# A list scheduler that orders a two-layer diffusion backbone 126 times instead of once, easing TensorE's longest pause each time

## The chip, the cores and the metric

One core of one Trainium2 chip runs the whole program. The metric is the device time of one execution in microseconds (us); the number that counts is the median of several runs. Engines are named as in the profile: PE is TensorE's matrix multiplication, PEld its weight load, DVE VectorE, ACT ScalarE, POOL GpSimd, SP the engine that issues all the transfers here.

## What is computed

A hybrid backbone of two layers over 512 latent and 256 context tokens of width 1024. Cut to what matters:

```python
for l in range(2):
    m_lat, m_ctx = silu(c) @ ada_w[l] + ada_b[l], silu(c_ctx) @ ada_w[l] + ada_b[l]     # 9 x 1024 each
    x, ctx = ffn_sublayer(x, m_lat[:, 0:3], ...), ffn_sublayer(ctx, m_ctx[:, 0:3], ...)  # FFN1
    mix_lat, mix_ctx = token_mix(modulate(x, ...), modulate(ctx, ...), w_in[l], w_out[l], ...)
    x = layer_norm(ALPHA * x + m_lat[:, 5] * mix_lat, ln_g[l, 1], ln_b[l, 1])
    x = ffn_sublayer(x, m_lat[:, 6:9], ...)                                              # FFN2
    # the context goes the same way in layer 0 alone
def modulate(x, shift, scale):  return layer_norm(x) * (1 + scale) + shift
def ffn_sublayer(x, m, w_gu, w_down, g, b):
    g_, u = split(modulate(x, m[0], m[1]) @ w_gu, 2)                                     # 1024 -> 2 x 2816
    return layer_norm(ALPHA * x + 0.5 * m[2] * (silu(g_) * u) @ w_down, g, b)
```

`token_mix` projects once (`w_in`) into three groups: grouped-query attention with RMS norm and rotation (A), a Hyena long convolution (B) and latent attention (C); their outputs are joined and projected by `w_out`.

## The kernel before

The tokens lie in six tiles of 128 (four latent, two context). Every 32-bit operand of the large products is split in two: a rounded part `hi`, cast by ACT, and the rest `lo`, subtracted by DVE or POOL; `mm3` then issues three matmuls (hi·hi, hi·lo, lo·hi). Weights come in tiles of 128x1024 through `weights`: SP loads `raw`, ACT casts `hi`, DVE subtracts `lo`.

Between two sublayers stands a path that no product can pass. `post` (L555) multiplies the output in PSUM with the gate and adds it to the residual (DVE, POOL), then normalises: `stats` (L507) takes `bn_stats` and `bn_aggr` on DVE and then a chain of 12 DVE steps on 128x2 values, variance plus epsilon, the ten steps of `rsqrt` (L490) and `nmr` (minus mean times the reciprocal root), each of which needs the one before. Two `scalar_tensor_tensor` of 128x1024 per tile apply it. `pre` (L535) then does `stats` again, with a second such chain, `norms` (L527) on ACT, transposes on PE, scale and shift on ACT, cast `Hhi` on ACT, and the rest `Hlo` on POOL. In the second half of layer 1 the latent tokens go through this in two groups of two tiles; the first three column blocks of FFN2 are made by `lat(..., cut=2)`, 144 matmuls of 128x256 for the first group and then 144 for the second.

Nothing is issued in the order in which the program names it. All engines are stand-ins (`_Engine`, L396) that record each operation with its dependencies and a cost by a formula (`cost`); this is why every instruction of the profile has the line L347. `order` then makes a list schedule: each engine in turn takes, of the operations that are ready by the modelled times, the one that comes first in the program. It models latencies between engines, the buffers of each pool (`_Slots`), the SBUF port that VectorE and GpSimd share (`shares`, `port`), and groups of matmuls that should stay together. `issue` emits the instructions in that order, and every engine keeps to it: an instruction that is not ready holds up all that stand behind it.

## Time and profile before

| | |
|---|---|
| median of 3 runs (lowest to highest) | 2902.86 us (2902.28 to 2903.89) |
| the profiled execution: its time, its span | 2903.62 us, 2901.2 us |
| PE busy, share of the span | 2812.3 us, 97% |
| DVE, ACT, POOL busy | 1716.4, 1006.4, 566.3 us |
| mean granted TensorE clock | 0.987 of 2.4 GHz |

The span is the time from the first to the last instruction of the execution, 2.4 us less than its device time. PE does nearly all the work, so that time lies in two things: pauses of PE (2901.2 less 2812.3, 88.9 us) and stretches in which its matmuls ran at 1.2 GHz (granted clock 0.5) instead of 2.4.

### The profile page before, as it was taken

The numbers are of one execution on the slowest core, as the hardware profiler recorded it, in microseconds if no ns is written. First come the engines' busy times: TensorE is split into PE (matmuls) and PEld (weight loads), VectorE is DVE, ScalarE is ACT, GpSimd is POOL, SyncE is SP. The second block draws the span as 40 slices with busy tenths as digits, with TensorE's granted clock in tenths as the row PEclk, the third lists the DMA queues.
The fourth block names the chain that finished last, engine by engine and source line by source line (L and its number), as shares of the span: only waits on it lengthen the run. The fifth ranks groups of instructions, "written<-read, shape, count | busy, mean of one in ns | idle before, by whom it ended". The sixth has DMA issues, their size and how long they took to land.

```text
span 2901.2 us, 41228 instructions
## 1 busy us (share of the span) xinstructions
PE 2812.3 (97%) x16132; PEld 2416.2 (83%) x16132; DVE 1716.4 (59%) x3485; ACT 1006.4 (35%) x1988; POOL 566.3 (20%) x545
## 2 busy tenths in 40 slices
PE   7999999999999999999999899999999999799998
PEld 5888888889887898888888788888889778688886
DVE  7887566286677663556626953653257677623335
ACT  4212222246657452121123421212217658432221
POOL 3201123125020031013311210122115220210220
PEclk9999999999999999999999999999999999899999
DMA  8654344121111313333321342431212113133231
GB/s 284 227 172 142 120 128 130 61 91 60 37 62 45 103 57 108 106 117 124 115 75 69 118 147 72 129 101 59 81 59 100 49 44 102 52 106 98 88 116 66
DMA packets 105714, 291.36 MB, mean 100 GB/s; under 512 B 15184, under 2 KB 17392, under 8 KB 105520
## 3 DMA queue, kind: packets, MB, share of 16 engines
q1 hardware_dynamic: 105520, 288.73, 30.7%
q8 instruction: 127, 2.08, 0.3%
q14 instruction: 67, 0.55, 0.1%
HBM read 277.23 MB, written 11.45 MB: 100 GB/s over the span
## 4 chain that ended last, share of the span: by engine, by line
PE 63%; DVE 5%; ACT 2%; issue 1%; POOL 0%; DVEq 0%; ACTq 0%; POOLq 0%
PE p L347 63%; DVE u L347 2%; DVE s L347 2%; ACT t L347 1%; DVE w L347 1%; DVE t L347 1%; ACT u L347 0%; ACT Hhi L347 0%; ACT w L347 0%; DVE Hlo L347 0%; DVE junk L347 0%; DVE adaw L347 0%; POOL Hlo L347 0%; ACT L347 0%; DVEq L1661 0%
## 5 line engine op out<-in xcount | busy, mean ns | idle before, releaser
L347 PE MATMUL p<-Hhi,w 128*128 128x256 f32 (+1 forms) x5536 | 1363.3, 337 | 9.3 <-ACT Hhi L347 6.1
L347 PEld LDWEIGHTS p<-Hhi,w 128*128 128x128 f32 x5536 | 953.8, 191 | 121.2 <-ACT Hhi L347 8.4
L347 PE MATMUL p<-Hlo,w 128*128 128x256 f32 (+1 forms) x2768 | 929.8, 336 | 0.1
L347 PE MATMUL p<-w,u 128*128 128x512 f32 x2904 | 665.7, 390 | 0.0
L347 DVE TENSOR_TENSOR w<-raw,w 128x1024 fp32r<-128x1024 f32 (+2 forms) x312 | 393.0, 1261 | 441.7 <-PE p L347 312.2
L347 PEld LDWEIGHTS p<-w,u 128*128 128x128 f32 x2904 | 543.7, 188 | 112.1
L347 ACT CAST w<-raw 128x1024 fp32r<-128x1024 f32 (+2 forms) x312 | 323.1, 1043 | 742.9 <-PE p L347 605.8
L347 PEld LDWEIGHTS p<-Hlo,w 128*128 128x128 f32 x2768 | 527.2, 191 | 53.8 <-issue 1.4
L347 POOL TENSOR_TENSOR u<-t,u 128x512 fp32r<-128x512 f32 (+1 forms) x154 | 185.7, 1206 | 1259.7 <-ACT u L347 1207.0
L347 DVE TENSOR_TENSOR t<-t,p 128x512 f32<-128x512 f32 (+1 forms) x160 | 90.9, 568 | 420.6 <-PE p L347 389.0
L347 PE MATMUL p<-u,u 128*64 128x128 f32 (+7 forms) x2120 | 277.4, 323 | 19.3 <-ACT t L347 5.2
L347 POOL TENSOR_TENSOR u<-u,t 128x512 f32<-128x512 f32 (+2 forms) x128 | 165.4, 1320 | 500.5 <-DVE t L347 366.7
L347 PEld LDWEIGHTS p<-u,u 128*64 128x64 f32 (+4 forms) x2120 | 202.8, 160 | 69.7 <-issue 27.0
L347 ACT CAST u<-t 128x512 fp32r<-128x512 f32 (+1 forms) x154 | 81.2, 528 | 410.4 <-DVE t L347 410.4
L347 DVE SCALAR_TENSOR_TENSOR junk<-adaw,crow 128x512 bf16<-128x512 f32 x256 | 209.5, 818 | 19.5 <-DMA adaw<-in_ada_t 18.6
L347 DVE SCALAR_TENSOR_TENSOR adaw<-adaw,crow 128x512 f32<-128x512 f32 x256 | 216.1, 844 | 7.0
L347 PE MATMUL p<-w,Hhi 128*128 128x416 f32 (+3 forms) x712 | 194.0, 354 | 6.7 <-ACT w L347 6.7
L347 DVE TENSOR_TENSOR t<-p,u 128x512 f32<-128x512 f32 x196 | 131.5, 686 | 91.2 <-PE p L347 90.1
L347 ACT ACTIVATE t<-p 128x512 f32<-128x512 f32 (+2 forms) x162 | 79.8, 495 | 291.2 <-PE p L347 286.9
L347 PEld LDWEIGHTS p<-w,Hhi 128*128 128x128 f32 x712 | 130.0, 193 | 18.3 <-ACT w L347 7.8
L347 PE MATMUL p<-ident,t 128*128 128x128 f32 x848 | 121.9, 282 | 22.2 <-ACT t L347 17.5
L347 POOL TENSOR_TENSOR Hlo<-t,Hhi 128x512 fp32r<-128x512 f32 x72 | 95.5, 1336 | 244.5 <-ACT Hhi L347 244.3
(122 smaller groups left out, 2181.2 us busy)
## 6 DMA issues: line engine op xcount, KB each, us to landing
raw<-in_ffn_gu SPq DMA_DIRECT2D x176, 512.0 KB, 3.6
adaw<-in_ada_t SPq DMA_DIRECT2D x256, 256.0 KB, 2.9
raw<-in_ffn_down SPq DMA_DIRECT2D x88, 512.0 KB, 3.6
raw<-in_w_out_u SPq DMA_DIRECT2D x16, 512.0 KB, 3.4
u<-in_x_all SPq DMA_DIRECT2D x12, 512.0 KB, 7.9
xs<-u SPq DMA_DIRECT2D x12, 512.0 KB, 2.7
raw<-in_w_hy SPq DMA_DIRECT2D x12, 512.0 KB, 3.3
u<-grow SPq DMA_DIRECT2D x10, 512.0 KB, 4.8
```

Source lines behind the costliest of these rows:

```text
L347: getattr(getattr(self.nc, eng), method)(*args, **kw)
```

## The change

The instructions of each engine are the same in number and kind. New is how often they are ordered, and what an order may do:

- `tune` makes the first schedule as before. Then it takes the longest modelled pause of TensorE above 150 ns (`gaps`) that it has not yet tried, and `hurry` walks back from the matmul that ends it, along what each operation waited for last, at most 12 us. For an operation on the way that was ready and had to wait over 60 ns for its engine it (1) gives it a priority ahead of those that ran in its way; (2) notes, in `behind`, big operations that had begun before it was ready, which must now come after it; (3) where the way leads through a chain of `stats`, adds this chain to `held`: once begun, VectorE takes nothing else until its 12 steps are done.
- Each such try is a new schedule: the priorities alone, the chains alone, all together. One is kept if the modelled end is earlier, up to 125 tries.
- `stats` keeps the scratch of `rsqrt` in the same tile as its other values (five columns per tile instead of four and a small tile of its own), and notes the chain by `nc.chain`.

```diff
+    PAUSE, BACK = 150.0, 12000.0
...
+    def chain(self, n0):
+        for n in range(n0, len(self.ops)):
+            self.chains[n] = n0
...
+    def gaps(self):
+        last, res = 0.0, []
+        for t, n in sorted((self.starts[n], n) for n, op in enumerate(self.ops) if op[0] == "tensor"):
+            if t - last > self.PAUSE:
+                res.append((t - last, n))
+            last = max(last, t + self.ops[n][6])
+        return sorted(res, reverse=True)
...
+    def hurry(self, n, prio, behind, held):
+        p, q, h, since = None, None, None, self.starts[n] - self.BACK
+        while n is not None and self.starts[n] > since:
+            t, r = self.starts[n], self.ready[n]
+            c = self.chains.get(n)
+            if c is not None and c not in held:
+                h = (h or held) | {c}
+            if t - r > 60.0:
+                x = prio[n]
+                for m in reversed(self.ran[self.ops[n][0]][:self.place[n]]):
+                    if self.starts[m] + self.ops[m][6] <= r:
+                        break
+                    x = min(x, prio[m] - 0.5)
+                    if self.starts[m] < r - 20.0 and self.ops[m][6] > 400.0 and self.ops[m][0] != "tensor":
+                        q = q or {k: [*v] for k, v in behind.items()}
+                        q.setdefault(n, []).append(m)
+                if x < prio[n]:
+                    p = p or [*prio]
+                    p[n] = x
+            n = self.cause[n]
+        return p or prio, q or behind, h or held
...
+    def tune(self, tries):
+        state = lambda: (self.end, self.starts, self.ready, self.cause, self.place, self.ran)
+        self.fixed = self.setup()
+        gc.disable()
+        now = [*map(float, range(len(self.ops)))], {}, frozenset()
+        res = self.order(*now)
+        kept = state()
+        done = set()
+        while tries > 0:
+            for _, n in self.gaps():
+                if n not in done:
+                    break
+            else:
+                break
+            done.add(n)
+            p, q, h = self.hurry(n, *now)
+            seen = [now]
+            for new in ((p, now[1], now[2]), (now[0], now[1], h), (p, q, h)):
+                if new in seen:
+                    continue
+                seen.append(new)
+                tries -= 1
+                r = self.order(*new)
+                if r and self.end < kept[0]:
+                    res, kept, now = r, state(), new
+                    done.discard(n)
+                    break
+                self.end, self.starts, self.ready, self.cause, self.place, self.ran = kept
+        gc.enable()
+        return res
...
-                if avail[e]:
+                    n = heapq.heappop(future[e])[1]
+                    heapq.heappush(avail[e], (prio[n], n))
+                if e == "vector" and hold is not None:
+                    t0 = max(when[e], ready[hold])
+                elif avail[e]:
...
+            if e == "vector" and hold is not None:
+                n = hold
+                avail[e].remove((prio[n], n))
+                heapq.heapify(avail[e])
+            else:
+                n = heapq.heappop(avail[e])[1]
...
-            if shares[n]:
+            if shares[n] and (e != "vector" or hold is None):
...
+            self.ready[n] = ready[n]
             for tag, r in opens[n]:
+                t1 = slots[tag].free[0]
+                if t1 > self.ready[n]:
+                    self.ready[n], cause[n] = t1, freed.get((tag, t1))
...
+                c = self.chains.get(n)
+                hold = n + 1 if c in held and self.chains.get(n + 1) == c else None
...
+            for m in behind.get(n, ()):
                 need[m] -= 1
...
     def issue(self):
-        for n in self.order():
+        for n in self.tune(125):
...
-    def rsqrt(self, y, v, t):
+    def rsqrt(self, y, v, t, p=None):
...
-        p = self.small(v.shape[-1])
+        if p is None:
+            p = self.small(v.shape[-1])
...
-        r = self.small(4 * n)
-        v, y, t, nmr = [r[:, n * i:n * i + n] for i in range(4)]
+        r = self.small(5 * n)
+        v, y, t, nmr, p = [r[:, n * i:n * i + n] for i in range(5)]
+        n0 = len(nc.ops)
         nc.vector.tensor_scalar(v, var, EPS, None, ALU.add)
-        self.rsqrt(y, v, t)
+        self.rsqrt(y, v, t, p)
         nc.vector.scalar_tensor_tensor(nmr, mean, -1.0, y, ALU.mult, ALU.mult)
+        nc.chain(n0)
         return [[x[:, j:j + 1] for x in (y, nmr, mean)] for j in range(n)]
```

What moves is seen in the order of the engines' instructions. In it the lines of the changed file are other ones (L465 for L347), and the numbers of the tiles are lower, since the scratch tiles are no longer named.

First, VectorE at the end of layer 1's token mix, where the first two latent tiles are normalised: s_3652 holds their mean and variance, s_3655 and s_3656 the chain's values; t and p with the numbers 367x are the gate's products of the other two tiles, w_3698 and w_3701 the `lo` parts of FFN2's weights. Before:

```order
L347 BN_AGGR s_3652<-s_3654 128x2
L347 TENSOR_SCALAR s_3655<-s_3652 128x2
L347 SCALAR_TENSOR_TENSOR u_3616<-u_3616,s_3652,u_3614 128x1024
L347 TENSOR_SCALAR s_3655<-s_3655 128x2
L347 SCALAR_TENSOR_TENSOR u_3617<-u_3617,s_3652,u_3614 128x1024
L347 TENSOR_SCALAR s_3655<-s_3655 128x2
L347 TENSOR_TENSOR t_3672<-p_3670,u_3613 128x512
L347 TENSOR_TENSOR s_3655<-s_3655 128x2
L347 SCALAR_TENSOR_TENSOR s_3655<-s_3655 128x2
L347 TENSOR_TENSOR w_3698<-raw_3696,w_3697 128x1024
L347 SCALAR_TENSOR_TENSOR s_3655<-s_3655 128x2
L347 BN_STATS s_3679<-u_3618 128x6
```

The same place now (the mean and variance are s_3625, the chain s_3628):

```order
L465 BN_AGGR s_3625<-s_3627 128x2
L465 TENSOR_SCALAR s_3628<-s_3625 128x2
L465 TENSOR_SCALAR s_3628<-s_3628 128x2 x2
L465 TENSOR_TENSOR s_3628<-s_3628 128x2
L465 SCALAR_TENSOR_TENSOR s_3628<-s_3628 128x2 x2
L465 TENSOR_TENSOR s_3628<-s_3628 128x2 x2
L465 TENSOR_SCALAR s_3628<-s_3628 128x2
L465 TENSOR_TENSOR s_3628<-s_3628 128x2
L465 SCALAR_TENSOR_TENSOR s_3628<-s_3628 128x2
L465 SCALAR_TENSOR_TENSOR s_3628<-s_3625,s_3628 128x2
L465 SCALAR_TENSOR_TENSOR u_3589<-u_3589,s_3625,u_3587 128x1024
L465 SCALAR_TENSOR_TENSOR u_3590<-u_3590,s_3625,u_3587 128x1024
```

The 12 steps stand in one piece, with what stood between them behind. The second chain of the same two tiles stands in one piece too, ahead of the other tiles' work and of the six weights' subtractions.

Second, PE at the same place: p_3675 (now p_3646) is the last of `w_out`'s sums, the matmuls with `ident` are the transposes of the first two tiles (t_3657, t_3658; now t_3629, t_3630), p_3702 the first sum of FFN2. Before:

```order
L347 MATMUL p_3675<-u_3648,Hhi 128x512
L347 MATMUL p_3675<-u_3649,Hhi 128x512
L347 MATMUL p_3675<-u_3648,Hlo 128x512
L347 MATMUL p_3665<-ident_83,t_3657 128x128 x4
L347 MATMUL p_3668<-ident_83,t_3658 128x128 x3
L347 MATMUL p_3666<-ident_83,t_3657 128x128 x4
L347 MATMUL p_3668<-ident_83,t_3658 128x128
L347 MATMUL p_3669<-ident_83,t_3658 128x128 x4
L347 MATMUL p_3702<-Hhi,w_3697 128x256
```

Now:

```order
L465 MATMUL p_3646<-u_3618,Hlo 128x512
L465 MATMUL p_3636<-ident_83,t_3629 128x128 x4
L465 MATMUL p_3646<-u_3618,Hhi 128x512
L465 MATMUL p_3639<-ident_83,t_3630 128x128 x4
L465 MATMUL p_3646<-u_3619,Hhi 128x512
L465 MATMUL p_3637<-ident_83,t_3629 128x128 x4
L465 MATMUL p_3646<-u_3618,Hlo 128x512
L465 MATMUL p_3640<-ident_83,t_3630 128x128 x4
L465 MATMUL p_3646<-u_3621,Hhi 128x512
```

The transposes stand among the last matmuls of `w_out`'s sum, nine of which follow the first four transposes, and no longer behind them all.

Third, VectorE in layer 1's input projection, where q of group A gets its RMS norm (the 128x12 values s_3138 to s_3141) and is scaled (t_3133): w_3242 and w_3289 are `lo` parts of weights, t_3157 a piece of Hyena's short convolution. Before:

```order
L347 TENSOR_SCALAR s_3139<-s_3139 128x12
L347 TENSOR_TENSOR w_3242<-raw_3240,w_3241 128x1024
L347 TENSOR_TENSOR s_3140<-s_3138,s_3139 128x12
L347 SCALAR_TENSOR_TENSOR t_3157<-p_3158,convw_3010,t_3157 128x511
L347 SCALAR_TENSOR_TENSOR s_3140<-s_3140,s_3139 128x12
L347 SCALAR_TENSOR_TENSOR t_3157<-p_3158,convw_3010,t_3157 128x511
L347 SCALAR_TENSOR_TENSOR s_3139<-s_3140,s_3139 128x12
L347 TENSOR_TENSOR s_3140<-s_3138,s_3139 128x12
```

Now:

```order
L465 TENSOR_SCALAR s_3112<-s_3112 128x12
L465 TENSOR_TENSOR s_3113<-s_3111,s_3112 128x12
L465 SCALAR_TENSOR_TENSOR s_3113<-s_3113,s_3112 128x12
L465 SCALAR_TENSOR_TENSOR s_3112<-s_3113,s_3112 128x12
L465 TENSOR_TENSOR s_3113<-s_3111,s_3112 128x12
```

The convolution's two pieces stand behind the scaling of q, and the subtraction of w_3242 (now w_3215) ten instructions further back still.

Two more places are spoken of below. On SP the first 512 KB of the modulation's weights (adaw_160) are loaded first of all and not fifteenth. And in the last 290 us of the program, all of FFN2 in layer 1 but its beginning, no engine's order changes.

## Rows read from the trace of the kernel before

**Rows 1.** The page: busy time of PE, and its busy tenths and clock in 40 slices.

```profile
PE 2812.3 (97%) x16132; PEld 2416.2 (83%) x16132; DVE 1716.4 (59%) x3485; ACT 1006.4 (35%) x1988; POOL 566.3 (20%) x545
...
PE   7999999999999999999999899999999999799998
...
PEclk9999999999999999999999999999999999899999
```

**Rows 2.** What PE waited for: us in total, times, longest.

```profile
PE p L347 <- ACT t L347: 26.6, 20, 10.3
PE p L347 <- DMA adaw<-in_ada_w: 10.1, 1, 10.1
```

**Rows 3.** Stretches: length; busy PE, PEld, DVE, ACT, POOL; clock, DMA share, GB/s.

```profile
0.00:45.00 45.00, 26.13 (x182) 13.11 (x182) 34.60 (x93) 23.87 (x38) 8.44 (x13) 1.00 0.87 312
636.00:662.00 26.00, 23.02 (x138) 21.19 (x137) 12.78 (x28) 20.52 (x51) 13.82 (x15) 0.94 0.17 64
850.00:950.00 100.00, 93.66 (x696) 77.74 (x694) 81.31 (x172) 63.34 (x179) 16.31 (x19) 0.98 0.15 48
1052.00:1593.00 541.00, 541.00 (x2997) 472.74 (x2997) 278.36 (x518) 135.56 (x215) 101.97 (x80) 1.00 0.30 98
1593.00:1645.00 52.00, 42.42 (x267) 36.04 (x266) 47.44 (x122) 28.67 (x60) 12.98 (x10) 0.87 0.30 94
...
2245.00:2300.00 55.00, 49.08 (x295) 40.27 (x293) 40.69 (x76) 31.77 (x70) 18.33 (x17) 0.91 0.19 64
2380.00:2436.00 56.00, 50.60 (x371) 40.57 (x371) 43.45 (x87) 38.01 (x100) 3.18 (x6) 0.95 0.15 48
2488.00:2548.00 60.00, 45.23 (x274) 41.23 (x273) 36.65 (x88) 28.00 (x54) 13.76 (x10) 0.83 0.14 45
2885.00:2901.00 16.00, 4.96 (x22) 3.75 (x20) 12.22 (x39) 0.00 (x0) 0.00 (x0) 0.80 0.26 98
```

**Rows 4.** PE's timeline, token mix to FFN2: start, us, instruction, count [idle before <-releaser].

```profile
2516.82 3.68 PE L347 MATMUL p<-ident,t 128*128 128x128 f32 x16 [10.28 <-ACT t L347]
2524.99 1.65 PE L347 MATMUL p<-Hhi,w 128*128 128x256 f32 x6 [4.49 <-ACT Hhi L347]
...
2529.81 0.36 PE L347 MATMUL p<-Hhi,w 128*128 128x256 f32 x1
...
2531.17 0.28 PE L347 MATMUL p<-Hlo,w 128*128 128x256 f32 x1
```

**Rows 5.** DVE's timeline at the same place.

```profile
2488.18 0.17 DVE L347 TENSOR_SCALAR s<-s 128x2 f32<-128x2 f32 x1
2488.26 1.28 DVE L347 SCALAR_TENSOR_TENSOR u<-u,s,u 128x1024 f32<-128x1024 f32 x1
...
2497.92 1.27 DVE L347 TENSOR_TENSOR s<-s,s 128x2 f32<-128x2 f32 x1
...
2502.46 2.47 DVE L347 BATCH_NORM_STATS2 s<-u 128x6 f32<-128x512 f32 x4
...
2516.17 0.36 DVE L347 TENSOR_TENSOR s<-s 128x2 f32<-128x2 f32 x2
```

**Rows 6.** ACT's timeline at the same place: `norms` of the first and second group.

```profile
2515.95 2.93 ACT L347 ACTIVATE t<-u,s 128x512 f32<-128x512 f32 x4 [12.63 <-DVE s L347]
...
2526.81 2.94 ACT L347 ACTIVATE t<-u,s 128x512 f32<-128x512 f32 x4 [0.17 <-DVE s L347]
```

**Rows 7.** POOL's timeline at the same place.

```profile
2496.93 2.24 POOL L347 TENSOR_TENSOR u<-u,t 128x512 f32<-128x512 f32 x1 [4.02 <-ACT w L347]
```

**Rows 8.** DVE's timeline, layer 1's projection: a weight's subtraction inside q's RMS chain.

```profile
2254.65 1.23 DVE L347 TENSOR_TENSOR w<-raw,w 128x1024 fp32r<-128x1024 f32 x1 [0.57 <-PE p L347]
```

**Rows 9.** PE's timeline where the scores of group A begin.

```profile
2279.67 1.19 PE L347 MATMUL p<-u,u 128*128 128x512 f32 x2 [3.86 <-DVE s L347]
```

**Rows 10.** DVE's timeline between layer 0 and layer 1: one step of a chain of `stats`.

```profile
1619.71 1.11 DVE L347 TENSOR_SCALAR s<-s 128x2 int32<-128x2 int32 x1
```

**Rows 11.** POOL's timeline at that step.

```profile
1619.54 1.26 POOL L347 TENSOR_TENSOR Hlo<-t,Hhi 128x512 fp32r<-128x512 f32 x1 [0.65 <-ACT Hhi L347]
```

More of the change, by code (lines that the diff above doesn't have):

```diff
@@ L1 @@
+import gc
 import heapq
@@ L67, in __init__ @@
         self.pools = {}
-        self.group = {}
+        self.group, self.chains = {}, {}
         for e in ("tensor", "vector", "scalar", "gpsimd", "sync"):
@@ L199, in shares @@
         return (two or bool(aps)) and not any(x.space == PSUM for x in args if isinstance(x, bass.AP))
-    def order(self):
+    def gaps(self):
[26 more added lines that the diff above has]
+        return p or prio, q or behind, h or held
@@ L202, in order, with setup @@
+    def setup(self):
         ops = self.ops
@@ L234, in order @@
                     opens[first[t]].append((tag, r))
-                slots[tag] = _Slots(tag[2], seq, self.AHEAD.get(tag[1], 16))
+                slots[tag] = tag[2], seq, self.AHEAD.get(tag[1], 16)
+        shares = [self.shares(*op[:4]) for op in ops]
+        return succ, need, left, opens, slots, rank, shares
+    def order(self, prio, behind, held):
+        ops = self.ops
+        N = len(ops)
+        cause = self.cause = [None] * N
+        self.ready = [0.0] * N
+        self.place = [0] * N
+        ran = self.ran = {e: [] for e in ("tensor", "vector", "scalar", "gpsimd", "sync")}
+        freed = {}
+        succ, need, left, opens, slots, rank, shares = self.fixed
+        need, left = [*need], {**left}
+        slots = {tag: _Slots(*x) for tag, x in slots.items()}
+        for n, ms in behind.items():
+            for m in ms:
+                need[m] += 1
         ends = {}
@@ L242, in order @@
         quiet, cold = -1e9, 0.0
-        tied = None
+        tied = hold = None
         port = {"vector": 0.0, "gpsimd": 0.0}
-        shares = [self.shares(*op[:4]) for op in ops]
         starts = self.starts = [0.0] * N
@@ L273, in order @@
                     best = (t0, e)
+            if best is None:
+                return None
             t0, e = best
@@ L276, in order @@
             while future[e] and future[e][0][0] <= t0:
[L277 to L278 removed]
+                n = heapq.heappop(future[e])[1]
+                heapq.heappush(avail[e], (prio[n], n))
+            if e == "vector" and hold is not None:
[4 more added lines that the diff above has]
+                n = heapq.heappop(avail[e])[1]
             if e == "tensor" and tied is not None and self.group.get(n) != tied:
[L281 to L283 removed]
+                for x in avail[e]:
+                    if self.group.get(x[1]) == tied:
+                        avail[e].remove(x)
                         heapq.heapify(avail[e])
[L285 to L286 removed]
+                        heapq.heappush(avail[e], (prio[n], n))
+                        n = x[1]
                         break
[L288 removed]
+            if shares[n] and (e != "vector" or hold is None):
                 free = port["gpsimd" if e == "vector" else "vector"]
@@ L292, in order @@
                     passed = [n]
-                    while avail[e] and len(passed) < 12 and shares[avail[e][0]]:
-                        passed.append(heapq.heappop(avail[e]))
-                    m = heapq.heappop(avail[e]) if avail[e] and not shares[avail[e][0]] else None
+                    while avail[e] and len(passed) < 12 and shares[avail[e][0][1]]:
+                        passed.append(heapq.heappop(avail[e])[1])
+                    m = heapq.heappop(avail[e])[1] if avail[e] and not shares[avail[e][0][1]] else None
                     for x in passed[m is None:]:
-                        heapq.heappush(avail[e], x)
+                        heapq.heappush(avail[e], (prio[x], x))
                     if m is not None:
@@ L307, in order @@
             res.append(n)
+            self.place[n] = len(ran[e])
+            ran[e].append(n)
             if shares[n]:
@@ L326, in order @@
                 lat = 0.0 if e == f == "tensor" else self.LAT["same" if e == f else "tensor" if "tensor" in (e, f) else "cross"]
-                ready[m] = max(ready[m], done + lat)
+                if done + lat > ready[m]:
+                    ready[m], cause[m] = done + lat, n
+                need[m] -= 1
+                if not need[m]:
+                    offer(m)
+            for m in behind.get(n, ()):
                 need[m] -= 1
@@ L336, in order @@
                     slots[tag].give(rank[t], ends[t] + self.LAT["cross"])
+                    freed[tag, ends[t] + self.LAT["cross"]] = n
                     wake.append(tag)
```

9 lines of the change are left out of this document (1 added, 8 removed).

## Prediction

> **What bounds the kernel now.** I read the page first: PE is busy for 97% of the span, its tenths are full nearly everywhere, and its clock is full but for one slice [rows 1]. So the kernel is bound by TensorE's own work, and a new order can only win what PE loses: 88.9 us of pauses (2901.2 - 2812.3) and the matmuls that ran at half clock. The second view, what PE waited for, says which pauses an order can reach: the largest sum, 26.6 us in 20 waits, is for ACT's `t`, the end of the path through the norms, while 10.1 us are one wait for the first weights by DMA [rows 2]. The third view, stretches, places them [rows 3]. In 1052 to 1593 PE has no pause at all, and the other long stretches between the rows look the same. Idle PE time (length less busy) is 18.9 us at the start, 3.0 in 636:662, 6.3 in 850:950, 9.6 in 1593:1645, 5.9 in 2245:2300, 5.4 in 2380:2436, 14.8 in 2488:2548 and 11.0 at the end. The clock tells of more: at 0.83 of 2488:2548, one third of that stretch was at 1.2 GHz (0.5) and the rest at 2.4.
>
> **The change, place by place.** Durations are of the profiled execution, 2903.62 us, 0.76 above the median; the sum is made against it.
>
> *Token mix to FFN2 in layer 1 (14.8 us idle).* Before, the first chain begins at 2488.18, each of its steps separated by foreign work of up to 1.28 us, and the four `bn_stats` behind it begin at 2502.46: 14.3 us [rows 5]. Held, 12 steps take 2.4 us (two steps take 0.36 and the next starts 0.39 after the first [rows 5], so 0.2 each), the four applications 4 x 1.2 = 4.8 us (1.28 each with 0.08 of overlap [rows 5]), so `bn_stats` begins at 2488.2 + 7.2 = 2495.4 and ends 2.4 later. Two aggregates and two gate products stand before the second chain (about 1.7 us by their like in these rows, an estimate), then 2.4 us of chain: `norms` starts at 2501.9, not at 2515.95 [rows 6], 14.0 us earlier. The first transposes could then run at 2516.8 - 14.0 = 2502.8 [rows 4], while `w_out`'s sum is still running; the wait of 10.28 goes. From the start of `norms` to FFN2's first matmul it took 9.04 us (2524.99 - 2515.95), through ACT and POOL, which stay: FFN2 starts at about 2511.0.
> What is late next is the second group. Its DVE work stands behind the chains and the six subtractions as before, so I leave its `norms` at 2526.8 [rows 6]; its first matmul then comes 9.04 later, at 2535.9. The first group's 144 matmuls at 0.12 us (0.36 from one triple to the next at full clock, behind [rows 4]) and 16 transposes at 0.09 last 18.7 us, to 2529.7: a new pause of 6 us. Before, the same work from 2524.99, its first 4.4 us at half clock, ended near 2546. The gain is 2546 - 2536 = 10, less 1 for a half-clock stretch behind the new pause: **-9** (bounds -5, if the chains meet POOL as told below and the second group comes later by what now passes it, and -12, if that group gains too).
>
> *Scores of group A in layer 1 (5.9 us idle, clock 0.91).* On DVE a subtraction of 1.23 us [rows 8] and two convolution pieces of 0.7 leave the RMS chain, so q is scaled 2.7 us earlier, and two more subtractions leave the time in which POOL rotates q. PE's wait of 3.86 [rows 9] is for what hangs on this. Convolution matmuls of later blocks are now fill between the scores. At clock 0.91, 0.18 of 55 us ran at half speed, 9.9 us, worth up to 5. I take **-6**; bounds -2 (2.7 less a stall of 0.7 at the transposes, which stand earlier) and -8.4 (all idle time and half the clock).
>
> *Layer 0 to layer 1 (9.6 us idle, clock 0.87).* The second of two chains is held; the first is not, and its 4 us stay. The `lo` subtraction that PE waited 2 us for comes earlier. **-4.4**; bounds -1 and -8.
>
> *FFN1 to token mix in layer 0 (3.0 us idle, clock 0.94).* The chain is held; at most 3.0 + 1.6 of clock. **-3.5**; bounds -1.5 and -4.5.
>
> *Small pauses in the attention of both layers (6.3 and 5.4 us).* Fill is moved in between them; half of 11.7: **-6**; bounds 0 and -10.
>
> *Unchanged.* Order is kept in the 541 us at full load and in the long stretches like it, and at the end (11.0 us idle). At the start the two DMA waits of 10.1 and 4.9 us stay in sum: one load of 512 KB passes the others at the 312 GB/s of that stretch [rows 3], 1.7 us that the others land later, while its own matmuls come earlier. I take 0, bounds -2 and +3.
>
> *What it costs.* PE changes between forms of operands 597 times and no longer 568, counted over its order. Where one matmul of a triple stands alone behind transposes, its successor starts 0.20 after it and not 0.12 (2529.81 and behind it [rows 4]): 29 x 0.08 = **+2.3**, bounds 0 and +3.
>
> Sum: -9 - 6 - 4.4 - 3.5 - 6 + 2.3 = -26.6; 2903.6 - 26.6 = 2877.0, at the median 2876.3. I forecast **2876 us**.
>
> **A rule that speaks against holding.** At 1619.71 a step on two values per partition takes 1.11 us, while POOL runs an operation from 1619.54 to 1620.80 [rows 10, 11]; at 2497.92 one takes 1.27, inside POOL's 2.24 [rows 5, 7]. Such a step takes 0.16 to 0.2 otherwise. So a held chain does not run at 0.2 us a step where POOL works, and DVE, kept from all other work, waits with it.
> The Trainium skill (SBUF — State Buffer, "SBUF: two separate sides") says the same as a mechanism: VectorE's operations with two SBUF inputs, or in a two-port mode, and GpSimd's share one pair of ports as an exclusive lock, and the loser is blocked for the whole operation of the other. By that rule alone no step of a chain is safe from POOL, and the sum would be that of the first rival; by the rows only steps that meet a POOL operation pay, and I take two of these on the path of the -9.
>
> **Rivals.**
> 1. *POOL stops the held chains, and the kernel gets slower.* Place: the four held chains on PE's path (two at 2488, one each in 636:662 and 1593:1645). Each blocked step costs 1.27 - 0.16 = 1.1 us; all 12 are 13.2 a chain, 53 in all, against a gain of 26.6: 2929. It decides at half of them, six blocked steps a chain (24 steps, 26.4 us). For it: four POOL operations lie in the chain's time in each of the two earlier places (15 and 10 in those whole stretches [rows 3]). Against it: between them POOL pauses for 0.65 us [rows 11], time for three steps, so that four operations block about four steps; and the interleaved chains of before paid for the same locks.
> 2. *What is gained is waited for at the next place.* The second group of FFN2, the rope of the A heads and the unheld chain each keep their time, and only the first part of each gain counts: -5, -2, -1, -1.5 and -1 are -10.5; with +2.3 the kernel is at 2894. For it: the new pause of 6 us is of this kind already. Against: 144 matmuls are a cover of 17 us.
> 3. *The pauses and the half-clock stretches behind them go altogether:* -12 - 8.4 - 8 - 4.5 - 10, with +2.3 and -2 at the start: -42.6, 2860. For it: 125 tries, each kept only if it helps the model; against it: ACT's and POOL's 9 us from `norms` to the first matmul stay in any order, and so does a pause behind each of them that finds no other work.
> 4. *Nothing measurable:* the order is shaped to modelled times, and where an operation comes later than modelled, PE, which takes its matmuls in order, stands before it with ready work behind. 2903.
>
> **How the numbers follow.** 0.2%, 5.8 us, is about what a measurement of this kernel tells from no change. Forecast 0.59, second rival 0.18 (a sixth of it within 0.2%), third 0.11, fourth 0.05, first 0.07. Faster 0.59 + 0.15 + 0.11 = 0.85, same 0.03 + 0.05 = 0.08, slower 0.07. The range reaches from 2856, a little below the third rival, to 2896, above the second; it leaves out the first and fourth and the tail of each side.
>
> **What would show it.** In the profile of the changed kernel: PE's longest wait behind the start no longer 10.28 for ACT's `t`, but one of 4 to 7 us between the two groups of FFN2; 12 chain steps in about 2.4 us at 2488, with at most two over 1 us; FFN2's first matmul under 6 us behind the end of `w_out`'s sum, not 18.5 (2524.99 less 2516.82 - 10.28); the wait of 3.86 at the scores under 1; the clock in the slice at 2500 above 0.9; the last 11 us as before. The forecast is wrong if a held chain takes over 6 us at 2488, if the transposes among `w_out`'s last matmuls hold PE for more than 3 us, or if the start takes 3 us more.

## The result and the profile after

The changed kernel takes **2873.68 us** (2872.49 to 2874.53, 4 runs) against 2902.57 (2901.67 to 2903.89, 4 runs): ratio 0.990, 95% interval 0.9883 to 0.9917, or 28.9 us less. The forecast was 2876.0, its range 2856 to 2896. The total came out as forecast; two of its terms did not, and two more lie a little past their bounds.

The page of the changed kernel, the lines of [rows 1] (lines of code are now L465):

```profile
PE 2803.5 (98%) x16132; PEld 2410.0 (84%) x16132; DVE 1721.2 (60%) x3485; ACT 1006.6 (35%) x1988; POOL 563.7 (20%) x545
...
PE   7999999999999999999999999999999999899998
...
PEclk9999999999999999999999999999999999999999
```

The span is 2871.7 us, so PE now pauses for 68.2 us and not 88.9: 20.7 of the 29.5 us by which the span shrank. The other 8.8 are PE's busy time, 2812.3 less 2803.5, with the same 16132 matmuls. The clock accounts for it: its mean rose from 0.987 to 0.991, and PE spent about 75 us of the span at 1.2 GHz before (0.013 x 2901.2 / 0.5) and about 52 now (0.009 x 2871.7 / 0.5). So nearly a third of the gain is matmuls that no longer run at 1.2 GHz.

What PE waited for, after:

```profile
PE p L465 <- ACT t L465: 17.1, 14, 4.8
PE p L465 <- ACT u L465: 8.8, 3, 7.8
PE p L465 <- DMA u<-in_hy_z: 6.5, 1, 6.5
PE p L465 <- ACT Hhi L465: 5.6, 2, 3.9
```

The largest sum is still for ACT's `t`, but 17.1 and not 26.6, and the longest of them is 4.8 and not 10.3 [rows 2]. Stretches of after, cut where the same work stands as in [rows 3], the first 45 us left for below:

```profile
639.30:660.60 21.30, 20.86 (x134) 19.82 (x132) 13.20 (x25) 18.94 (x47) 11.22 (x12) 1.00 0.19 72
848.30:944.40 96.10, 92.15 (x696) 76.45 (x694) 80.09 (x171) 63.51 (x179) 15.71 (x19) 1.00 0.15 48
1045.40:1586.50 541.10, 541.10 (x2998) 472.80 (x2997) 281.72 (x531) 130.79 (x202) 97.02 (x76) 1.00 0.31 98
1586.50:1633.20 46.70, 40.11 (x265) 34.91 (x264) 39.30 (x105) 27.88 (x60) 11.55 (x9) 0.85 0.30 94
2234.40:2276.00 41.60, 38.91 (x210) 31.34 (x209) 31.91 (x57) 23.89 (x46) 16.31 (x17) 1.00 0.27 84
2355.60:2409.60 54.00, 51.53 (x392) 42.03 (x390) 43.37 (x87) 38.44 (x99) 5.42 (x8) 1.00 0.15 50
2461.60:2518.50 56.90, 47.25 (x278) 42.58 (x277) 40.73 (x87) 27.56 (x54) 13.49 (x10) 0.89 0.14 47
2855.50:2871.50 16.00, 5.00 (x23) 3.79 (x21) 12.26 (x39) 0.00 (x0) 0.00 (x0) 0.78 0.26 98
```

The full stretch (1045 to 1586) and the end are as before. In four places the clock is 1.00 where it was 0.94, 0.98, 0.91 and 0.95. Two places still run at 0.85 and 0.89. Not all of this is the change's: in run 1 below, whose order on PE, DVE, ACT and POOL is that of before, the clock between 850 and 950 is 1.00 as well.

**Where the time went, place by place.** I matched every matmul of the two traces and took the difference of its start at points of PE's order behind which the same set of matmuls stands in both. What the difference grows by between two points is what that place gave:

| place (us of before) | forecast (bounds) | measured |
|---|---|---|
| start, to 97 | 0 (-2 to +3) | +3.3 |
| FFN1 to token mix, layer 0 (620 to 665) | -3.5 (-4.5 to -1.5) | -4.7 |
| small pauses, attention of layer 0 (850 to 950) and layer 1 (2375 to 2450) | -6 (-10 to 0) | -3.9 and -6.4 |
| layer 0 to layer 1 (1593 to 1656) | -4.4 (-8 to -1) | -5.3 |
| scores of A, layer 1 (2245 to 2310) | -6 (-8.4 to -2) | -7.7 |
| token mix to FFN2, layer 1 (2486 to 2561) | **-9 (-12 to -5)** | **-3.0** |
| changes between operand forms | +2.3 (0 to +3) | not seen apart |
| rest: -0.3 (665 to 850), -0.9 (at 1050), +1.2 (at 2181), -1.8 (2310 to 2375) | 0 | -1.8 |
| sum, against the profiled execution (measured: its span) | -26.6 | -29.5 |

Between 2260 and 2389 the order has no common point; there I gave each matmul's own gain to its place in before, so the split of these 13.6 us into -7.7, -1.8 and -4.1 is an estimate, their sum is not. The table sets one execution against one. How much a place changes without any change of order is seen in run 1: -0.7 between 620 and 665, -1.4 between 850 and 950, under 0.3 at each other place behind the start.

**Token mix to FFN2.** DVE's timeline of after; a row with xN puts N like instructions together:

```profile
2461.73 0.58 DVE L465 TENSOR_SCALAR s<-s 128x2 f32<-128x2 f32 x3
...
2463.92 0.16 DVE L465 SCALAR_TENSOR_TENSOR s<-s,s 128x2 f32<-128x2 f32 x1
2464.00 4.87 DVE L465 SCALAR_TENSOR_TENSOR u<-u,s,u 128x1024 f32<-128x1024 f32 x4
...
2472.49 2.33 DVE L465 TENSOR_SCALAR s<-s 128x2 f32<-128x2 f32 x3
...
2482.54 2.12 DVE L465 TENSOR_TENSOR w<-raw,w 128x1024 fp32r<-128x1024 f32 x1
2484.57 1.75 DVE L465 TENSOR_TENSOR u<-u,t 128x512 f32<-128x512 f32 x1
2486.24 2.30 DVE L465 TENSOR_TENSOR w<-raw,w 128x1024 fp32r<-128x1024 f32 x1
...
2489.07 1.69 DVE L465 TENSOR_TENSOR w<-raw,w 128x1024 fp32r<-128x1024 f32 x1
...
2501.51 0.58 DVE L465 TENSOR_SCALAR s<-s 128x2 f32<-128x2 f32 x3
```

POOL's timeline at the same place, and ACT's (`norms` of the two groups):

```profile
2472.05 2.54 POOL L465 TENSOR_TENSOR u<-u,t 128x512 f32<-128x512 f32 x2 [21.79 <-DVE s L465]
2482.30 1.27 POOL L465 TENSOR_TENSOR Hlo<-t,Hhi 128x512 fp32r<-128x512 f32 x1 [7.71 <-ACT Hhi L465]
2484.22 3.24 POOL L465 TENSOR_TENSOR Hlo<-t,Hhi 128x512 fp32r<-128x512 f32 x2 [0.65 <-ACT Hhi L465]
2488.29 1.38 POOL L465 TENSOR_TENSOR Hlo<-t,Hhi 128x512 fp32r<-128x512 f32 x1 [0.83 <-ACT Hhi L465]
```

```profile
2476.71 2.93 ACT L465 ACTIVATE t<-u,s 128x512 f32<-128x512 f32 x4 [4.59 <-DVE s L465]
...
2503.96 2.23 ACT L465 ACTIVATE t<-u,s 128x512 f32<-128x512 f32 x3 [15.74 <-DVE s L465]
```

PE's timeline there:

```profile
2481.49 0.40 PE L465 MATMUL p<-u,Hlo 128*128 128x512 f32 x1
2485.76 1.43 PE L465 MATMUL p<-Hhi,w 128*128 128x256 f32 x5 [3.87 <-ACT Hhi L465]
...
2506.50 1.04 PE L465 MATMUL p<-ident,t 128*128 128x128 f32 x8
2509.39 0.66 PE L465 MATMUL p<-ident,t 128*128 128x128 f32 x4 [1.86 <-ACT t L465]
2511.65 0.66 PE L465 MATMUL p<-ident,t 128*128 128x128 f32 x4 [1.60 <-ACT t L465]
2514.07 1.65 PE L465 MATMUL p<-Hhi,w 128*128 128x256 f32 x6 [1.76 <-ACT Hhi L465]
```

And before, DVE's timeline at the second group's second chain:

```profile
2522.37 0.58 DVE L347 TENSOR_SCALAR s<-s 128x2 f32<-128x2 f32 x3
...
2523.17 1.40 DVE L347 SCALAR_TENSOR_TENSOR s<-s 128x2 f32<-128x2 f32 x2
...
2525.20 1.12 DVE L347 TENSOR_TENSOR s<-s,s 128x2 f32<-128x2 f32 x1
```

This place begins 26.45 us earlier than before; add that to compare. The first chain takes 2461.73 to 2464.08, 2.35 us for its 12 steps. In the second, three steps that took 0.58 take 2.33: they meet POOL's two adds, and it lasts 4.1. `norms` of the first group starts at 2476.71 + 26.45 = 2503.16, 12.8 us earlier than 2515.95 [rows 6], and FFN2's first matmul comes at 2512.21, 12.8 earlier than [rows 4] and 3.87 behind the last of `w_out`'s.

The second group lost. Its `norms` starts at 2503.96 + 26.45 = 2530.41 against 2526.81 [rows 6], **3.6 us late**. The first group's `Hlo` adds on POOL now fall where DVE does the work ahead of the second group's chain: three subtractions take 2.12, 2.30 and 1.69 where they take 1.2 [rows 8], and an add 1.75 where its like at 2477.71 takes 0.68: 0.9 + 1.1 + 0.5 + 1.1 = 3.6.

That this sum equals the delay is in part chance. The second group's second chain begins 5.6 us late (2501.51 + 26.45 against 2522.37). Besides the 3.6, the two blocked steps of the first group's second chain cost 1.75, and the held chains slow DVE itself: a step of a held chain takes 0.2 us, while one between foreign work holds that work up for 0.08 (2488.18 to 2488.26 [rows 5]); for 24 steps that is 2.9, an estimate. Against it stands what before lost in the same stretch, a wait of 1.29 (at 2493.03) and a step blocked for 1.1 [rows 5]. Then 2.0 come back, for the second group's second chain now takes 2.35 us, where before two of its steps met POOL's adds (the rows above) and it took 4.34.

### The profile page after: what moved, and what is told of

Its sections match the earlier page's. It is cut to its first block, busy times and chain, and to the rows that moved or that the text cites. A ratio compares the mean times of both kernels' runs of the same rounds, so it can differ in the third digit from the quotient of the medians.

```text
span 2871.7 us, 41216 instructions
## 1 busy us (share of the span) xinstructions
PE 2803.5 (98%) x16132; PEld 2410.0 (84%) x16132; DVE 1721.2 (60%) x3485; ACT 1006.6 (35%) x1988; POOL 563.7 (20%) x545
## 4 chain that ended last, share of the span: by engine, by line
PE 89%; DVE 7%; ACT 3%; issue 1%; DMA 0%; SPq 0%; POOL 0%; DVEq 0%; ACTq 0%; POOLq 0%
PE p L465 89%; DVE u L465 3%; DVE s L465 3%; ACT t L465 2%; DVE t L465 1%; DVE w L465 0%; ACT u L465 0%; DMA cc<-in_cc 0%; ACT Hhi L465 0%; ACT w L465 0%; SPq L465 0%; ACT L465 0%; DVE Hlo L465 0%; DVE adaw L465 0%; DVE junk L465 0%
## 5 line engine op out<-in xcount | busy, mean ns | idle before, releaser
L465 PE MATMUL p<-Hhi,w 128*128 128x256 f32 (+1 forms) x5536 | 1367.8, 337 | 8.3 <-ACT Hhi L465 5.6
L465 PEld LDWEIGHTS p<-Hhi,w 128*128 128x128 f32 x5536 | 955.9, 191 | 120.6 <-ACT Hhi L465 6.3
L465 PE MATMUL p<-Hlo,w 128*128 128x256 f32 (+1 forms) x2768 | 931.0, 337 | 0.0
L465 PE MATMUL p<-w,u 128*128 128x512 f32 x2904 | 665.5, 390 | 0.0
L465 DVE TENSOR_TENSOR w<-raw,w 128x1024 fp32r<-128x1024 f32 (+2 forms) x312 | 392.9, 1261 | 410.9 <-PE p L465 311.0
L465 PEld LDWEIGHTS p<-w,u 128*128 128x128 f32 x2904 | 543.6, 188 | 112.1
L465 ACT CAST w<-raw 128x1024 fp32r<-128x1024 f32 (+2 forms) x312 | 323.2, 1043 | 726.9 <-PE p L465 598.2
L465 PEld LDWEIGHTS p<-Hlo,w 128*128 128x128 f32 x2768 | 528.2, 191 | 53.5 <-issue 1.5
L465 POOL TENSOR_TENSOR u<-t,u 128x512 fp32r<-128x512 f32 (+1 forms) x154 | 185.4, 1204 | 1254.8 <-ACT u L465 1185.1
L465 DVE TENSOR_TENSOR t<-t,p 128x512 f32<-128x512 f32 (+1 forms) x160 | 90.9, 568 | 421.0 <-PE p L465 391.7
L465 PE MATMUL p<-u,u 128*64 128x128 f32 (+7 forms) x2120 | 272.1, 319 | 12.4 <-DMA u<-in_hy_z 6.5
L465 POOL TENSOR_TENSOR u<-u,t 128x512 f32<-128x512 f32 (+2 forms) x128 | 164.0, 1310 | 506.6 <-DVE t L465 417.4
L465 PEld LDWEIGHTS p<-u,u 128*64 128x64 f32 (+4 forms) x2120 | 197.8, 156 | 60.1 <-issue 22.7
L465 DVE SCALAR_TENSOR_TENSOR junk<-adaw,crow 128x512 bf16<-128x512 f32 x256 | 216.7, 846 | 21.6 <-DMA adaw<-in_ada_t 19.8
L465 ACT CAST u<-t 128x512 fp32r<-128x512 f32 (+1 forms) x154 | 81.4, 529 | 403.1 <-DVE t L465 403.1
L465 DVE SCALAR_TENSOR_TENSOR adaw<-adaw,crow 128x512 f32<-128x512 f32 x256 | 208.0, 812 | 7.2
L465 PE MATMUL p<-w,Hhi 128*128 128x416 f32 (+3 forms) x712 | 192.2, 352 | 6.9 <-ACT w L465 6.8
L465 DVE TENSOR_TENSOR t<-p,u 128x512 f32<-128x512 f32 x196 | 130.9, 685 | 93.6 <-PE p L465 92.3
L465 ACT ACTIVATE t<-p 128x512 f32<-128x512 f32 (+2 forms) x162 | 80.0, 496 | 299.5 <-PE p L465 299.5
L465 PEld LDWEIGHTS p<-w,Hhi 128*128 128x128 f32 x712 | 129.2, 191 | 18.5 <-ACT w L465 7.5
L465 POOL TENSOR_TENSOR Hlo<-t,Hhi 128x512 fp32r<-128x512 f32 x72 | 96.1, 1346 | 239.7 <-ACT Hhi L465 239.5
L465 ACT COPY u<-p 128x512 f32<-128x512 f32 (+4 forms) x225 | 112.9, 533 | 57.5 <-PE p L465 52.6
```

The lines of the kernel that those rows point to most:

```text
L465: getattr(getattr(self.nc, eng), method)(*args, **kw)
```

## Experiments

All but the first take the tables that the search ends with (`prio`, 61 priorities that differ from program order; `behind`, 14 entries; `held`, five chains), edit them, and make one schedule from them; of each edit only the lines that differ are shown. Numbers are positions of operations in the recorded program. The ratios are to the kernel before as it was measured with each run (medians from 2901.67 to 2902.36). All calls in `issue` read so:

```diff
-        for n in self.tune(125):
+        for n in self.pick():
```

**1. The first schedule alone, with the new scratch tile.**

```diff
+    def pick(self):
+        return self.tune(0)
```

> The first schedule alone, without any try, with the scratch of rsqrt in the tile of its chain: on PE, DVE, ACT and POOL the order of the kernel before, on SP 15 transfers between 1035 and 1645 us stand otherwise. Theory (the new order does it all): 2902.6 us, within 1.5. Rival (fewer small tiles free DVE from waits for a buffer): under 2899.

Measured 2902.26 (2900.11 to 2906.49), ratio 1.000 (0.9991 to 1.001). The tile is worth nothing by itself; all that follows is order.

**2. The held chains alone.**

```diff
+        prio, behind, held = self.now
+        return self.order([*map(float, range(len(self.ops)))], {}, held)
```

> Only the five chains are held; no priority is changed, nothing is put behind. The order differs from before only around FFN1 to token mix of layer 0, 1035 us on, layer 0 to layer 1, and token mix to FFN2 of layer 1. Theory (each place keeps its own gain, and chains carry the gain at the norms): -4 at the first, -0.5, -2.5 at the third, -3 at the last: about 2892, from 2889 to 2895. Rival (what makes the norms early is the priorities on ACT and the weights, and chains alone move DVE's waiting elsewhere): 2898 to 2903.

Measured 2887.49 (2885.86 to 2888.54), ratio 0.9946 (0.9931 to 0.9961): 15 us, more than either theory gave. By place, where the order differs: -3.9 (620 to 665), -0.9 (1053), -3.7 (1593 to 1671), -4.0 (FFN2, its first matmul again 12.8 earlier, its second group 5.6), together -12.5 where -10 was expected. Of the rest, -1.5 (850 to 950) and -3.2 (2260 to 2450) lie where the order is that of before; the clock of 2380 to 2436, 0.95 before [rows 3], was 1.00 there in this execution. So part of this run's gain is a difference between executions.

**3. The priorities and `behind` alone, no chain held.**

```diff
+        prio, behind, held = self.now
+        return self.order(prio, behind, frozenset())
```

> The 61 priorities and the 14 operations put behind, with no chain held. Theory (places add): all of the change but what the chains give: +3.3 at the start, -5 in layer 0's attention, -2 to -3 between the layers, -15 between 2195 and 2450: about 2883, from 2880 to 2886, and the gains of this run and of the run with the chains alone add up to the whole -29 within 2. Rival (they work together, the priorities only on top of the chains): the two sum to less than 24.

Measured 2887.00 (2886.01 to 2889.23), ratio 0.9946 (0.9931 to 0.9961). By place: start +5.7, 620 to 665 -1.8, attention of layer 0 -3.9, 1593 to 1656 +2.3, 2245 to 2389 -13.8, 2390 to 2450 -2.3, FFN2 -0.3. That is 1 us past the expected range; its start took 2.4 us more than expected. So FFN2 is the held chains' alone, and the scores are the priorities'. Against 2902.36, measured with them, runs 2 and 3 save 14.9 and 15.4, together 30.2 where the whole saves 28.9. In sum the parts add up, as the theory had it, but not place by place: between the layers (1593 to 1656) the chains alone give -3.7 and the priorities alone +2.3, while both together give -5.3. There the priorities pay only on top of the chains, as the rival had it.

**4. The change without its one moved load** (the priority on SP).

```diff
+        prio = [float(n) if eng == "sync" else x for n, (x, (eng, *_)) in enumerate(zip(prio, self.ops))]
```

> The change without its one priority on SP: the first 512 KB of the modulation's weights are loaded fifteenth again, and the order of the first 130 us is that of before on every engine; nothing else moves. Theory (the start costs 3.3 us, for its waits are as long as before, but fall in three late pauses behind which PE runs 6.8 us at half clock): 2870.4 us, from 2869.5 to 2871.5, and no half-clock stretch between 38 and 45 us. Rival (the start's loss is hidden later, where PE waits for other things): 2873.7, as the change.

Measured 2870.76 (2870.27 to 2873.89), ratio 0.9892 (0.9876 to 0.9909), as the theory had it: the start stands at -0.65 instead of +3.3. But a half-clock stretch stays, against the theory. The stretch before the clock recovers, before, after and in this run:

```profile
34.00:45.00 11.00, 8.42 (x78) 5.11 (x78) 10.96 (x15) 10.26 (x19) 7.62 (x6) 1.00 0.61 229
```

```profile
34.00:45.00 11.00, 7.79 (x46) 4.03 (x44) 6.39 (x11) 8.73 (x17) 6.59 (x7) 0.69 0.63 226
```

```profile
34.00:45.00 11.00, 9.45 (x71) 5.34 (x69) 10.51 (x13) 9.32 (x18) 8.27 (x6) 0.84 0.64 233
```

The clock of 0.69 means 6.8 us of these 11 at 1.2 GHz (0.31 x 11 / 0.5), that of 0.84 means about 3.5. Of the five profiled executions with the load in its old place, the one before has no such stretch and the other four (runs 1, 2, 4 and 10) have one at 0.84; all eight with the moved load have twice that. So the kernel before, in the execution that I forecast from, was the lucky one. The pauses in the first 45 us sum to 18.9 before, 18.7 after and 17.3 here. The moved load makes the first one 6.48 and not 4.88, and late ones bunch, as PE's timeline of after shows:

```profile
35.92 0.44 PE L465 MATMUL p<-ident,u 128*128 128x128 f32 x2 [1.34 <-ACT t L465]
...
39.32 1.02 PE L465 MATMUL p<-sel,t 128*128 128x2 f32 x4 [1.14 <-DVE t L465]
```

By the matching of matmuls, the start costs between 2.6 and 6.9 us in the eight executions with the move, and between -0.7 and +0.8 in the others.

**5. The second group of FFN2 first.** One subtraction of weights waits for the start of its first chain, three for the end of its second, which is held.

```diff
+        for n, ms in ((18972, [19058]), (19005, [19061, 19064, 19067])):
+            behind.setdefault(n, []).extend(ms)
+        return self.order(prio, behind, held | {18994})
```

> The change, and in it the last four of the six weight subtractions that stood ahead of the second group's chains at FFN2 in layer 1 are put behind: w_3607 behind the start of its first chain, the other three behind the end of its second, which is held. Theory (the second group's norms are 3.6 us late because six subtractions, stretched by POOL, pass them): its norms start 5 to 6 us earlier, the three pauses of 1.86, 1.60 and 1.76 us between the groups go and so does the half-clock stretch behind them: 2867, from 2865.5 to 2869. Rival (the first group's matmuls then wait for these weights instead): 2872 to 2875, with PE waiting on DVE's w inside the first group.

Measured 2871.07 (2869.75 to 2871.37), ratio 0.9892 (0.9877 to 0.9907): less than half of what was expected. FFN2 gives -6.4 and not -3.0. Its DVE timeline and then PE's:

```profile
2487.37 1.23 DVE L475 TENSOR_SCALAR s<-s 128x2 int32<-128x2 int32 x1
...
2489.71 1.24 DVE L475 TENSOR_SCALAR s<-s 128x2 int32<-128x2 int32 x1
```

```profile
2502.09 1.42 PE L475 MATMUL p<-ident,t 128*128 128x128 f32 x8 [2.60 <-ACT t L475]
```

The chain's steps moved forward into the time of POOL's `Hlo` adds and paid there (1.23 and 1.24 for 0.16); `norms` came 3.5 us earlier, but the transposes stood too early in PE's order, and PE waited 2.60 with ready matmuls behind. Of the half-clock stretch, which was to go, half stays (3.4 us from 2503.3).

**6. POOL's two adds behind the first group's second chain.**

```diff
+        behind.setdefault(18817, []).extend([18911, 18913])
```

> The change, and in it the two additions of POOL that lie over the first group's second chain at FFN2 in layer 1 (two of its steps take 0.88 and 1.21 us there) come behind this chain. Theory (POOL's lock stretches the chain, but the end is set by the second group): the 12 steps take 2.4 us and not 4.0, the first group's norms start 1.5 us earlier, and the time stays at 2873.7 within 1, as the second group is as late as before. Rival (the first group is on the path): 2872.2 or less; second rival (the additions now meet the second group's two-input work): 2875 or more.

Measured 2874.68 (2873.70 to 2876.89), ratio 0.9906 (0.9892 to 0.9921). Inconclusive: the note orders the schedule, but POOL, which keeps its own queue, took the adds as soon as their inputs were there, 0.44 us ahead of the chain (2472.72 against 2473.16) as in the changed kernel (2472.05 against 2472.49), and the same three steps took 2.33 again. An edit of the order binds only within an engine.

**7. The same, by holding back what the adds read**: the two gate products on DVE, and two subtractions, stand behind the chain.

```diff
+        behind.setdefault(18817, []).extend([18910, 18912, 19052, 19055])
```

> The change, and in it the two gate products on DVE that start POOL's two additions, and the first two weight subtractions, come behind the first group's second chain at FFN2 in layer 1 (in the run before, POOL's additions were only named later and still ran at once). Theory (POOL's lock stretches the chain from 2.4 to 4.0 us, and the end is set by the second group): all 12 steps at 0.2 us, the first group's norms about 2 us earlier, the time the same within 1 us of 2873.7. Rival (the first group is on the path): 2872 or less.

Measured 2872.73 (2871.15 to 2876.68), ratio 0.9901 (0.9887 to 0.9914). DVE's and POOL's timelines:

```profile
2473.42 0.57 DVE L474 TENSOR_SCALAR s<-s 128x2 f32<-128x2 f32 x3
...
2475.60 0.16 DVE L474 SCALAR_TENSOR_TENSOR s<-s,s 128x2 f32<-128x2 f32 x1
```

```profile
2476.53 3.52 POOL L474 TENSOR_TENSOR u<-u,t 128x512 f32<-128x512 f32 x2 [26.53 <-DVE t L474]
```

With POOL idle all 12 steps take 0.2 us, 2.3 in all; so POOL was what stretched them. On what bounds this place the run says less than it was to. Two later subtractions took the freed time ahead of the chain, so that the first group's `norms` came only 0.6 us earlier and not 2, while the second group's came 1.6 earlier; the place gives -5.2 in the profiled execution and not -3.0, 1.0 of it at the second group's first matmul and the rest in a half-clock stretch of 3.4 us and not 6.8. The median is 0.95 below the change, within the spread of these four executions. That the second group bounds the place is shown by runs 5 and 10, which at this place change only what stands ahead of that group's chains.

**8. Without six priorities near 2170**, 80 us before the scores.

```diff
+        prio = [float(n) if 15800 < n < 16300 else x for n, x in enumerate(prio)]
```

> The change without its six priorities at 2169 to 2180 (five matmuls of one projection and the cast of w_2925). DVE's order at 2252 to 2275 is then that of before, with the weights' subtractions inside q's RMS chain again; the priority on the scores' maximum at 2275 stays. Theory (the gain of 13.8 between 2245 and 2340 comes with the subtractions that leave q's chain, a by-product of a move 80 us earlier): 2882 to 2887. Rival (it comes from the maximum's priority): 2872 to 2875.

Measured 2885.65 (2884.57 to 2886.55), ratio 0.9943 (0.9928 to 0.9958). DVE's and PE's timelines at the scores:

```profile
2245.11 1.23 DVE L473 TENSOR_TENSOR w<-raw,w 128x1024 fp32r<-128x1024 f32 x1 [0.55 <-PE p L473]
```

```profile
2269.53 1.19 PE L473 MATMUL p<-u,u 128*128 128x512 f32 x2 [2.66 <-DVE u L473]
```

The subtraction is back in q's chain [rows 8], and so is most of the wait [rows 9]: up to before's 2342 nothing is left of the gain. PE's order up to the scores is that of before again as well, so this run does not separate the subtraction from the fill that the change puts between the scores; run 9 keeps both (q's chain takes 3.5 us there as in after, and 6.4 here as before), and the gain there. In after, PE's timeline has only this there:

```profile
2259.24 0.70 PE L465 MATMUL p<-u,u 128*128 128x512 f32 x2 [0.51 <-DVE u L465]
2261.73 0.73 PE L465 MATMUL p<-Hhi,w 128*128 128x512 f32 x2 [1.55 <-DVE w L465]
2264.40 1.43 PE L465 MATMUL p<-u,u 128*128 128x512 f32 x6 [0.56 <-ACT t L465]
```

So the largest gain of the change hangs on a move 80 us earlier: weights prepared at 2170 to 2180 leave q's chain free. There the move itself gains nothing and costs next to nothing: that place stands at +1.2 with it, at +0.9 without it in this run, and at +0.8 in run 2, which has no priorities.

**9. Without the priority on the scores' maximum** (near 2275).

```diff
+        prio = [float(n) if n == 16983 else x for n, x in enumerate(prio)]
```

> The change without its priority on the scores' maximum at 2275 alone; the subtractions stay outside q's chain. Theory (as in the run before): 2873.7 to 2876. Rival: 2882 or more.

Measured 2886.03 (2884.55 to 2887.72), ratio 0.9943 (0.9926 to 0.9959), a miss. The scores kept their gain (-12.2 to 2386), as the theory had it, but the order behind them changed, and between 2389 and 2440, where the change gains 2.3, this kernel lost 6.5 us to new pauses of up to 1.94 and a clock of 0.94 in that stretch. Another 3.6 of the difference stand at the start, whose order is the same: PE's first wait, for its first load, is 8.5 us here and 6.5 in after. Why one small operation turns the order 100 us later was not settled.

**10. A better one: the moved load undone, two subtractions behind the start of the second group's first chain, two behind the end of its second.**

```diff
+        prio = [float(n) if op[0] == "sync" else x for n, (x, op) in enumerate(zip(prio, self.ops))]
+        for n, ms in ((18972, [19058, 19061]), (19005, [19064, 19067])):
+            behind.setdefault(n, []).extend(ms)
+        return self.order(prio, behind, held | {18994})
```

> The two repairs together: the start as before, and at FFN2 in layer 1 the subtractions of w_3607 and w_3610 behind the start of the second group's first chain, the other two behind the end of its second, which is held. Theory (places add): -3.0 at the start and -3.4 to -4.6 at FFN2: 2866.5, from 2865 to 2868. Rival (the later weights stop the first group's matmuls): 2870.

Measured **2865.94** (2865.77 to 2866.07), ratio 0.9875 (0.9862 to 0.9889): better than both kernels. Its PE timeline between the groups:

```profile
2500.07 0.66 PE L476 MATMUL p<-ident,t 128*128 128x128 f32 x4 [1.03 <-ACT t L476]
...
2508.26 0.98 PE L476 MATMUL p<-Hhi,w 128*128 128x256 f32 x6 [0.93 <-ACT Hhi L476]
```

FFN2 gives -8.3, close to the -9 of the forecast. The 5.2 us between the groups are now 2.3, in three pauses of at most 1.03, and the second stretch at half clock is gone: the matmul at 2508.26 has 0.98 for its six, not 1.65.

**11. One more chain held** (the one left free between the layers, at 1601).

```diff
+        return self.order(prio, behind, held | {11941})
```

> The change with one more chain held, the first of the two before layer 1's FFN1 (at 1601 us before). Theory (this chain, interleaved with foreign work, ends in PE's wait of 4.77 us and in 6.8 us at half clock): the chain takes 2.4 to 4 us and not 8.6, the wait is under 1.5, and the time is 2869.5, from 2868 to 2872. Rival (what passes it makes the other tiles' chain as much later): 2873 to 2875.

Measured 2880.91 (2879.09 to 2882.42), ratio 0.9929 (0.9915 to 0.9943): 7 us slower than the change, where 4 faster were expected. PE's and DVE's timelines:

```profile
1623.94 3.59 PE L474 MATMUL p<-ident,t 128*128 128x128 f32 x16 [3.84 <-ACT t L474]
1632.65 1.01 PE L474 MATMUL p<-Hhi,w 128*128 128x256 f32 x3 [4.08 <-ACT Hhi L474]
```

```profile
1619.15 0.69 DVE L474 TENSOR_TENSOR t<-t,p 128x512 f32<-128x512 f32 x1 [1.96 <-POOL u L474]
```

The chain itself did as meant: PE's wait there fell from 4.77 to 1.44. But the chain behind it starts 8 us later than in the changed kernel, with DVE idle for 1.96 in front of a gate product that was not ready, and PE waits 3.84 and 4.08 for it. The place gives 5 us less than in the changed kernel. That is the second rival of the prediction, shown with one more chain: what is gained at one place is waited for at the next.

## Why the prediction was right, and where it was not

- **The bound, right.** PE's work is the kernel; the change could only win pauses and clock, and of 29.5 us it won 20.7 and 8.8.
- **Holding a chain, right.** 12 steps in 2.35 us in the first chain, two blocked steps and 4.1 us in the second; runs 2 and 3 show that FFN2's gain is this alone. `norms` of the first group 12.8 us earlier (14.0 forecast), first matmul of FFN2 at 2512.2 (2511.0), 3.87 behind `w_out` (under 6), and between the groups 1.86 + 1.60 + 1.76 = 5.2 us (4 to 7, but in three pauses and not one). PE's longest wait behind the start is now 4.77, between the layers.
- **The term of -9, wrong: -3.0.** The step that failed is "I leave its `norms` at 2526.8": it came at 2530.4. With these 3.6 us, and 10.1 and not 9.04 from `norms` to the first matmul (2514.07 - 2503.96), the second group's first matmul is 5.6 us earlier than before, where I had 10; the half-clock stretch behind the pause then took 2.5, and I had taken 1. I had priced POOL's locks on the held chains, but not on the subtractions that the earlier `Hlo` adds would meet, and I had let the held chains take no more of DVE's time than the interleaved ones. Runs 5 and 10 bear it out: with four of these subtractions put behind, the place gives -6.4 and -8.3.
- **Scores, mechanism right.** -7.7 within the bounds. Run 8, with the subtraction back in q's chain, has lost the gain; PE's order changes with it, so the fill between the scores may have its share. My -6 gave the clock too little: at 0.91 before, 1.00 after.
- **Small pauses, too small: -10.3, not -6.** I took half of 11.7 idle us and left out their clock, 0.98 and 0.95 before and 1.00 after. Of the -3.9 in layer 0, run 1 has 1.4 with the order of before.
- **Start, wrong: +3.3, not 0.** The step that failed is that equal pauses cost the same: their sum stayed, as forecast, and the first load is 1.6 later, against 1.7; but the pauses bunch, and 6.8 us at half clock stand there, where the execution before had none (run 4). It is also one of the three signs by which the forecast called itself wrong, a start that takes 3 us more; the other two did not come.
- **Layer 0 to 1 and FFN1 to token mix, right:** -5.3 for -4.4 and -4.7 for -3.5, the second 0.2 past its bound. The mechanism of the first is only half shown, since neither part alone gives it (run 3).
- **Form changes:** a cost of 2.3 would be hidden in the other rows; no run takes it apart.

So that the total is right within 3 us is in part luck: two errors one way (6.0 at FFN2, 3.3 at the start) stand against several the other way: 8.1 in the four terms that gave more, 1.8 in places not named, and the 2.3 booked for forms.

The first rival, POOL's locks, is real and small: in the four held chains that it named 8 of 48 steps are blocked (none and two in FFN2, three in each of the other two), where 24 would have decided. By the rule of the Trainium skill (SBUF — State Buffer, "SBUF: two separate sides") the loser is blocked for the whole of the other's operation; the traces agree, since the blocked step of [rows 10] ends at 1620.82 and POOL's add [rows 11] at 1620.80, and in run 7, with POOL idle, the steps take 0.2 each. The three subtractions above lose 0.5 to 1.1 us each where they meet POOL's adds. The second rival is what happened to FFN2 in part, and run 11 shows it outright; its sum comes to 2894.7 at the median and not 2894, which changes nothing.

## What to carry to other kernels

When work moves forward, follow the engine that it frees next: POOL's adds moved with the first group, and where they met the second group's DVE work they cost it 3.6 us. A held chain is paid for by what waits behind it: its steps took 0.2 us each of DVE's time, and holding one more chain cost 7 us (run 11). In a kernel that one engine fills, read the clock with the pauses: nearly a third of this gain was clock. A change of order is judged by its place and by what stands behind it (runs 8, 9 and 11), and a place by more than one execution: with the same order, one place differed by 1.4 us (run 1), and the start by 3.6 (run 9).

## What was not expected of the hardware

- The clock fell to 1.2 GHz behind short pauses, but not always. In after, pauses of 1.34, 0.23 and 0.50 us between 34.6 and 37.5 stand ahead of 6.8 us at 1.2 GHz from 38.1 on, and 1.86 and 1.60 ahead of 6.8 us from 2512.8 on; 1.03, 0.93 and 0.38 in run 10 had none behind them. With one and the same order and pauses of about 0.5 to 0.6 us, the clock fell for 3.4 us at 38.3 in run 1, and not at all there before. What decides it was not settled.
- One load of 512 KB moved ahead makes the first of all loads land later by an amount that changes from run to run: PE's first wait is 6.2 to 8.5 us in the eight profiled executions with the move, and 4.9 to 5.1 in the five without it.
